# Operand addresses, three more U products ahead, ranks' products on VectorE and another pace of gathers in a PEER layer

## The chip, the cores and the metric

One core of a Trainium2 chip runs the program. The metric is the device time of one execution in microseconds (us): 1605.35 us is the median of three runs of the kernel before (1603.85 to 1605.81).

## What is computed

One encoder layer on 512 tokens of width 1024: a mixer (in-projection, an RG-LRU group, a convolution group, out-projection), then PEER, a retrieval over 128 x 128 single-neuron experts, and a final norm. All is fp32. The part that fills most of the time is PEER:

```python
def peer_ffn(n, w_q, sub_keys, expert_u, expert_v):       # per block of 128 tokens
    q = einsum("td,de->te", xt, w_q)                        # 8 heads x 2 halves x 128
    s = einsum("thpc,hpkc->thpk", q, sub_keys)
    s1, i1 = top_k(s[:, :, 0], 16);  s2, i2 = top_k(s[:, :, 1], 16)
    cand_s = s1[..., :, None] + s2[..., None, :];  cand_i = i1 * 128 + i2
    top_s, pos = top_k(cand_s, 16);  idx = take_along_axis(cand_i, pos);  gate = softmax(top_s)
    act = gelu(einsum("thkd,td->thk", expert_u[idx], xt))
    return einsum("thk,thkd->td", gate * act, expert_v[idx])
```

## The kernel before

**Two ways for the experts.** The first 384 tokens are done densely: all 16384 experts in 128 groups of 128. For group i a *U product* gives gelu(U_i x) for 128 experts x 384 tokens (`dense_u`, L447: 24 matmuls of 384 columns, L452 to L454), the gates are multiplied in (`weigh`, L704), and a *V product* adds V_i times that into six PSUM banks that stay open to the end (`dense_v`, L725: 18 matmuls of 512 columns, L731). The last 128 tokens are done by gathering: 128 (head, rank) pairs, for each a row of U per token and later a row of V per token, 256 "shares" in all. A share is one indirect DMA on POOL's queue into a `g_t` buffer (L655) and one DVE instruction over 128 x 1024 (dots L667, sums L677).

**Precision by splitting.** Each fp32 matrix is loaded by SP's queue into one of five `raw_t` buffers (L94) and split into two fp32r parts: `w_hi` by ACT (L99), `w_lo` by DVE or POOL (L101, the caller chooses). Each product is then three matmul series. The activations are split once, into `m_hi` and `m_lo`.

**Stages.** 0 to about 322 us: mixer. *Routing* to 502.6 us: for the 16 half-heads a query product (`query`, L551, its `w_lo` on POOL), scores, and `rank` on DVE; after half-heads 3, 7 and 11 `choose` (L491) for two heads, after 13 and 15 for one. `choose` finds ranks' keys by comparing with an iota (`eq`, L526 on DVE, 2048 elements for two heads, 1024 for one), multiplying by the index (L528 on POOL, in place) and summing (L530 on DVE), twice. The 22 U products of this stage have their `w_lo` on POOL. *Scatter* to about 680 us: 24 steps build the dense gates by one-hot products (`hot` L623, `oa` L627 on DVE, L633 on PE), write them to memory `scr_g`, and make one U product each, with `w_lo` on DVE, up to U45. *Transition*: gates come back as `g_s` tiles of eight groups (`load_gates`, L699, two buffers), the U products still missing to 48 are made, `w_lo` on POOL. *Main loop* (L750): V0 to V127; in the turns i = 4 to 83 also U(i + 44). *Tail*: the last three V products bank by bank, the norms, the output.

**Homes and pace.** A U product made ahead lives in a home tile until its V product: eight halves of the `g_t` buffers (U0 to U7), 15 `w_e`, 26 `w_f`; HOMES = AHEAD_U + 1 - 8 = 41 in the ring, LAG = 4. The gathers keep a pace: after turn i, `256 * pace(i + 1) // pace(116)` shares are issued, where a turn with U and V counts 2 and one with V alone 1: 2.61 shares in a turn with both, 1.31 in one with V alone, and the last at i = 115.

**Who sets the order.** Each engine runs its own instructions strictly in order; Tile's scheduler fixes that order when the program is built, from the dependences and its own estimate of times. Multiplications by gates (L705) are so drawn far ahead of the loop's turns.

Of the kernel before, what the change touches and what calls it, by code (L numbers as in the profile page):

```python
# [53 lines left out]
SELN = P + 2 + P  # L54


@with_exitstack
def tile_kernel(ctx, tc, x, par, wi, bd, kd, mg, wo, wq, keys, u_rows, v_rows, u_t, v_t, fg, ffg, sel, out):
    nc = tc.nc
# [371 lines left out]
    wk = ctx.enter_context(tc.tile_pool(name="wk", bufs=1))  # L433
    ps_e = ctx.enter_context(tc.tile_pool(name="ps_e", bufs=2, space=PSUM))

    AHEAD_U = 48
    AHEAD_W = 2
    EARLY = 2
    us = {}
# [2 lines left out]
    HOMES_NOW = 15  # L442

    LAG = AHEAD_U - HOMES - 3
    homes = [(wk, "w_e", HOMES_NOW)]

    def dense_u(i, eng):  # L447
        hi, lo = split(load(u_t[i].rearrange("p c e -> p (c e)")), eng)
        p = ps_e.tile([P, TD], F32, name="p_e")
        for c in range(NC):  # L450
            cs = slice(c * P, (c + 1) * P)
            nc.tensor.matmul(p, hi[:, cs], m_hi[:, c, :TD], start=(c == 0), stop=False)  # L452
            nc.tensor.matmul(p, hi[:, cs], m_lo[:, c, :TD], start=False, stop=False)  # L453
            nc.tensor.matmul(p, lo[:, cs], m_hi[:, c, :TD], start=False, stop=(c == NC - 1))  # L454
        if i < len(spare):
            w = spare[i]
        else:
            pool, name, n = homes[(i - len(spare)) % HOMES >= HOMES_NOW]
            w = pool.tile([P, NT, GT], F32, name=name, bufs=n)
        nc.scalar.activation(flat(w), p, AF.Gelu_apprx_tanh)  # L460
        us[i] = w
# [29 lines left out]
    def choose(rp, v, i, g, keys_, h0, n):  # L491
# [32 lines left out]
        for t in range(2):  # L524
            eq = rp.tile(big, BF16, name="eq")
            nc.vector.tensor_tensor(eq, pb[:, t].unsqueeze(1).to_broadcast(big), ioj[:, :, 0:m, :],  # L526
                                    op=ALU.is_equal)
            nc.gpsimd.tensor_tensor(eq, eq, ii[:, :, t, :].rearrange("p h j -> p j h").unsqueeze(3)  # L528
                                    .to_broadcast(big), op=ALU.mult)
            nc.vector.tensor_reduce(merge(keys_[:, t, hh]), eq.rearrange("p j h k -> p h k j"),  # L530
                                    axis=AX.X, op=ALU.add)
# [51 lines left out]


    wk2 = ctx.enter_context(tc.tile_pool(name="wk2", bufs=1))
    homes.append((wk2, "w_f", HOMES - HOMES_NOW))
    TURN = 4
    GS = 8

# [18 lines left out]
    def scatter(b, trb):  # L608

        ahead = None  # L610
        shp = [P, GS // SB, NK, SB]
        for t0 in range(0, P, GT):
            stg = bp.tile([P, NK, GT], F32, name="stg", bufs=2)
            for t1 in range(0, GT, GS):

                def over(q):
                    return (trb[:, q, t0 + t1:t0 + t1 + GS].rearrange("p (g t) -> p g t", t=SB).unsqueeze(2)
                            .to_broadcast(shp))

                hot = []  # L620
                for q in (0, 1):
                    o = bp.tile(shp, BF16, name=f"hot{q}", bufs=2)
                    nc.vector.tensor_tensor(o, iot.unsqueeze(1).to_broadcast(shp), over(q), op=ALU.is_equal)  # L623
                    hot.append(o)
                oa = bp.tile([P, 3] + shp[1:], BF16, name="oa", bufs=2)
                for q in range(3):
                    nc.vector.tensor_tensor(oa[:, q], hot[1], over(2 + q), op=ALU.mult)  # L627
                for t2 in range(0, GS, 4):
                    p = ps_g.tile([P, 4, NK], F32, name="p_g")
                    for t in range(4):  # L630
                        g, o = divmod(t2 + t, SB)
                        for q in range(3):
                            nc.tensor.matmul(p[:, t, :], hot[0][:, g, :, o], oa[:, q, g, :, o],  # L633
                                             start=(q == 0), stop=(q == 2))
                    o = t1 + t2
                    nc.scalar.activation(stg[:, :, o:o + 4], p.rearrange("p t k -> p k t"), AF.Copy)
            nc.sync.dma_start(scr_g[(b * P + t0) // GT], flat(stg))
            if t0 == TURN * GT and b < DB - 1:
                ahead = turned(b + 1)
            if len(us) < AHEAD_U:  # L640
                dense_u(len(us), nc.vector)
        return ahead

# [106 lines left out]
    for i in range(NK):  # L750
# [96 lines left out]
```

## Time and profile before

| what | us |
|---|---|
| median of three runs | 1605.35 |
| the profiled execution | 1603.43 |
| its span (first to last instruction) | 1601.7 |
| PE busy | 1491.6 |
| DVE / POOL / ACT busy | 1225.9 / 649.4 / 637.3 |
| mean granted TensorE clock | 0.964 of 2.4 GHz |

A busy time is the time in which at least one instruction ran on the engine. A wait names what came last before the waiting instruction could start. A profile row of form "A <- B: total, times, longest" is the idle time of A that ended with B.

### The profile page before, as it was taken

How to read it: one execution, taken by the hardware profiler on the slowest of the kernel's cores; microseconds unless marked ns; L12 is line 12 of the kernel's file. 1: busy time of each engine (PE TensorE's matmuls, PEld its weight loads, DVE VectorE, ACT ScalarE, POOL GpSimd, SP SyncE). 2: the span in 40 equal slices, each digit the busy share in tenths (PEclk: the TensorE clock that was granted, in tenths of full speed). 3: DMA queues.
4: the chain of work that ended last, by engine and by line, in shares of the span. 5: the costliest groups of instructions: out<-in, count | busy, mean ns of one | idle time of the engine just before them, and what ended most of it. 6: DMA issues, size and time to landing. Idle time of an engine off the chain costs nothing.

```text
span 1601.7 us, 21647 instructions
## 1 busy us (share of the span) xinstructions
PE 1491.6 (93%) x7939; PEld 1299.6 (81%) x7939; DVE 1225.9 (77%) x2296; ACT 637.3 (40%) x937; POOL 649.4 (41%) x388
## 2 busy tenths in 40 slices
PE   5987989988987999977999999999999999999997
PEld 4754757878877999967888899889998899888886
DVE  6995645398899999937987777777777877777765
ACT  5367453334334554522333333333333333333333
POOL 3644723465572000224444555454444544444410
PEclk9998979999998999998999999999999999999999
DMA  6210503321322555598998988989989898878762
GB/s 230 91 65 15 196 14 132 105 79 67 106 70 102 213 221 211 190 286 305 365 377 304 328 299 310 328 282 334 324 305 334 287 327 286 293 285 296 284 234 79
DMA packets 137787, 358.69 MB, mean 224 GB/s; under 512 B 10064, under 2 KB 59472, under 8 KB 134352
## 3 DMA queue, kind: packets, MB, share of 16 engines
q1 hardware_dynamic: 100240, 222.03, 40.4%
q0 software_dynamic: 36864, 134.23, 22.8%
q8 instruction: 62, 1.02, 0.3%
q10 hardware_dynamic: 576, 1.05, 0.2%
q14 instruction: 45, 0.37, 0.1%
HBM read 327.91 MB, written 29.36 MB: 223 GB/s over the span
## 4 chain that ended last, share of the span: by engine, by line
PE 59%; DVE 7%; DMA 3%; issue 2%; POOL 1%; ACT 0%; DVEq 0%; ACTq 0%; POOLq 0%
PE po L731 31%; PE p_e L454 8%; PE p_e L452 8%; PE p_e L453 8%; PE p_g L633 3%; DVE oa L627 2%; DMA g_t<-in_u_rows,eidx 2%; DMA g_s<-scr_g 2%; DVE hot L623 1%; DVE w_lo L101 1%; DVE g_t L667 0%; POOL g_t L655 0%; DVE key_d L530 0%; DVE w_f L705 0%; DMA raw_t<-in_u_t 0%
## 5 line engine op out<-in xcount | busy, mean ns | idle before, releaser
L99 ACT CAST w_hi<-raw_t 128x1024 fp32r<-128x1024 f32 x302 | 316.1, 1050 | 426.6 <-PE p_e L453 257.5
L454 PE MATMUL p_e<-m_hi,w_lo 128*128 128x384 f32 x1024 | 349.9, 342 | 10.7 <-DVE w_lo L101 10.7
L452 PE MATMUL p_e<-m_hi,w_hi 128*128 128x384 f32 x1024 | 352.2, 344 | 7.0 <-ACT w_e L460 6.2
L453 PE MATMUL p_e<-m_lo,w_hi 128*128 128x384 f32 x1024 | 348.1, 340 | 0.1
L101 POOL TENSOR_TENSOR w_lo<-raw_t,w_hi 128x1024 fp32r<-128x1024 f32 x70 | 177.2, 2543 | 321.3 <-ACT w_hi L99 303.9
L101 DVE TENSOR_TENSOR w_lo<-raw_t,w_hi 128x1024 fp32r<-128x1024 f32 x232 | 280.4, 1219 | 25.1 <-ACT w_hi L99 25.0
L655 POOL DMA_INDIRECT g_t<-in_u_rows,eidx x128 | 197.9, 1546 | 240.8 <-DVE g_t L667 195.5
L655 POOL DMA_INDIRECT g_t<-in_v_rows,eidx x128 | 187.8, 1467 | 222.7 <-DVE acc L677 211.8
L731 PE MATMUL po<-w_hi,wt_hi 128*128 128x512 f32 x768 | 242.8, 395 | 8.9 <-ACT wt_hi L707 8.9
L731 PE MATMUL po<-w_lo,wt_hi 128*128 128x512 f32 x768 | 243.0, 395 | 0.8 <-DVE w_lo L101 0.8
L731 PE MATMUL po<-w_hi,wt_lo 128*128 128x512 f32 x768 | 243.1, 395 | 0.0
L454 PEld LDWEIGHTS p_e<-m_hi,w_lo 128*128 128x128 f32 x1024 | 196.3, 192 | 12.7 <-DVE w_lo L101 12.7
L452 PEld LDWEIGHTS p_e<-m_hi,w_hi 128*128 128x128 f32 x1024 | 196.4, 192 | 11.6 <-ACT w_e L460 6.9
L453 PEld LDWEIGHTS p_e<-m_lo,w_hi 128*128 128x128 f32 x1024 | 196.4, 192 | 4.2 <-DVE m_lo L133 0.4
L667 DVE SCALAR_TENSOR_TENSOR g_t<-g_t,Xg 128x1024 f32<-128x1024 f32 x128 | 152.3, 1221 | 32.4 <-DMA g_t<-in_u_rows,eidx 32.4
L731 PEld LDWEIGHTS po<-w_lo,wt_hi 128*128 128x128 f32 x768 | 143.9, 187 | 36.9 <-DVE w_lo L101 1.5
L731 PEld LDWEIGHTS po<-w_hi,wt_hi 128*128 128x128 f32 x768 | 143.1, 188 | 37.3 <-ACT wt_hi L707 9.2
L731 PEld LDWEIGHTS po<-w_hi,wt_lo 128*128 128x128 f32 x768 | 143.8, 187 | 35.8 <-DVE wt_lo L709 0.4
L677 DVE SCALAR_TENSOR_TENSOR acc<-g_t,dots,acc 128x1024 f32<-128x1024 f32 x127 | 162.3, 1278 | 0.0
L709 DVE TENSOR_TENSOR wt_lo<-w_f,wt_hi 128x384 fp32r<-128x384 f32 x75 | 42.0, 560 | 112.5 <-ACT wt_hi L707 110.2
L707 ACT CAST wt_hi<-w_f 128x384 fp32r<-128x384 f32 x75 | 38.6, 515 | 205.3 <-PE po L731 202.9
L627 DVE TENSOR_TENSOR oa<-hot,trb 128x1024 bf16<-128x1024 bf16 x144 | 90.6, 681 | 0.0
(214 smaller groups left out, 1937.9 us busy)
## 6 DMA issues: line engine op xcount, KB each, us to landing
raw_t<-in_u_t SPq DMA_DIRECT2D x128, 512.0 KB, 5.9
raw_t<-in_v_t SPq DMA_DIRECT2D x128, 512.0 KB, 5.9
scr_g<-stg SPq DMA_DIRECT2D x24, 1024.0 KB, 4.3
g_s<-scr_g SPq DMA_DIRECT2D x16, 1536.0 KB, 16.0
raw_t<-in_wi SPq DMA_DIRECT2D x16, 512.0 KB, 3.9
raw_t<-in_wq SPq DMA_DIRECT2D x16, 512.0 KB, 3.7
raw_t<-in_wo SPq DMA_DIRECT2D x8, 512.0 KB, 5.5
raw_t<-in_kd SPq DMA_DIRECT2D x6, 512.0 KB, 3.7
```

Source lines behind the costliest of these rows:

```text
L99: nc.scalar.copy(hi, t)
L101: eng.tensor_sub(lo, t, f(hi))
L452: nc.tensor.matmul(p, hi[:, cs], m_hi[:, c, :TD], start=(c == 0), stop=False)
L453: nc.tensor.matmul(p, hi[:, cs], m_lo[:, c, :TD], start=False, stop=False)
L454: nc.tensor.matmul(p, lo[:, cs], m_hi[:, c, :TD], start=False, stop=(c == NC - 1))
L627: nc.vector.tensor_tensor(oa[:, q], hot[1], over(2 + q), op=ALU.mult)
L633: nc.tensor.matmul(p[:, t, :], hot[0][:, g, :, o], oa[:, q, g, :, o], start=(q == 0), stop=(q == 2))
L655: nc.gpsimd.indirect_dma_start(out=t, out_offset=None, in_=rows, in_offset=bass.IndirectOffsetOnAxis(ap=eidx[:, k // K, k % K:k % K + 1], ...
L667: nc.vector.scalar_tensor_tensor(t, t, 1.0, Xg, op0=ALU.mult, op1=ALU.mult, accum_out=dots[:, k:k + 1])
L677: nc.vector.scalar_tensor_tensor(acc, t, dots[:, k:k + 1], acc, op0=ALU.mult, op1=ALU.add)
L709: return whi, wlo, nc.vector.tensor_sub(wlo, flat(w), f(whi))
L731: nc.tensor.matmul(po[b][hf], lhs[:, bs], rhs[:, hf * 512:(hf + 1) * 512], start=(i == 0 and n == 0), stop=(i == NK - 1 and n == 2))
```

## The change

Four edits.

1. **Addresses.** `ones` grows from 1 to 32 floats a partition, and a tile `eps_` of 8 floats that nothing reads is put at the other end of SBUF. The tiles behind them (`m_hi`, `m_lo`, `raw_t`, `w_hi`, `w_lo`, `w_e`, `w_f` on one side; `g_t`, `wt_hi`, `wt_lo`, `stg`, `oa`, `eq` on the other) then begin at 0 instead of 32 modulo 64 bytes. Some tiles of the mixer (`recur`'s, the out-projection's `w_hi` and `w_lo`, `h_t`) go from 0 to 32. Two memsets are added.
2. **51 U products ahead** instead of 48: the ring has 44 homes, three of them (`w_g`) in memory that the scatter frees. The scatter still makes U up to U45; the transition makes five (U46 to U50) instead of two; the loop makes 77 instead of 80, in turns 4 to 80.
3. **The ranks' products** (L528, ten instructions: six of 2048 elements, four of 1024) go from POOL to DVE.
4. **Pace.** No share in the first four turns, 7 parts in a turn with U and V, 3 in one with V alone, over `pace(123)` = 7 x 77 + 3 x 42 = 665 parts: 2.69 shares, then 1.155, and the last at i = 122.

```diff
-    ones = keep.tile([P, 1], F32, name="ones")
-    nc.vector.memset(ones, 1.0)
+    ones_ = keep.tile([P, ONEW], F32, name="ones")
+    nc.vector.memset(ones_, 1.0)
+    ones = ones_[:, 0:1]
...
+    edge = ctx.enter_context(tc.tile_pool(name="edge", bufs=1, side="right"))
+    eps_ = edge.tile([P, 8], F32, name="eps_")
+    nc.vector.memset(eps_, EPS)
...
-    AHEAD_U = 48
+    AHEAD_U = 51
...
-            pool, name, n = homes[(i - len(spare)) % HOMES >= HOMES_NOW]
+            k = (i - len(spare)) % HOMES
+            pool, name, n = homes[(k >= HOMES_NOW) + (k >= HOMES - HOMES_END)]
...
-            nc.gpsimd.tensor_tensor(eq, eq, ii[:, :, t, :].rearrange("p h j -> p j h").unsqueeze(3)
+            nc.vector.tensor_tensor(eq, eq, ii[:, :, t, :].rearrange("p h j -> p j h").unsqueeze(3)
...
-            if len(us) < AHEAD_U:
+            if len(us) < AHEAD_U - HOMES_END - 2:
...
-        return i + min(max(i - LAG, 0), NK - AHEAD_U)
+        n = min(max(i - LAG, 0), NK - AHEAD_U)
+        return 7 * n + 3 * max(i - LAG - n, 0)
...
+    wk3 = ctx.enter_context(tc.tile_pool(name="wk3", bufs=1))
+    homes.append((wk3, "w_g", HOMES_END))
...
-            done = 2 * H * K * pace(i + 1) // pace(NK - 12)
+            done = 2 * H * K * pace(i + 1) // pace(NK - 5)
```

**What moves in the queues.** Line numbers of the changed kernel are 9 to 14 higher (L101 is L110, L526 is L537, L528 is L539, L530 is L541, L705 is L717, L709 is L721, L667 is L678). POOL's queue at the first `choose`, before:

```order
L101 TENSOR_TENSOR w_lo<-raw_t,w_hi 128x1024 x2
L533 TENSOR_TENSOR gate_d<-ts 128x128
L538 TENSOR_TENSOR gate_d<-gate_d,den 128x128
L528 TENSOR_TENSOR eq<-eq,ii 128x2048 x2
L101 TENSOR_TENSOR w_lo<-raw_t,w_hi 128x1024 x6
```

After:

```order
L110 TENSOR_TENSOR w_lo<-raw_t,w_hi 128x1024 x2
L544 TENSOR_TENSOR gate_d<-ts 128x128
L549 TENSOR_TENSOR gate_d<-gate_d,den 128x128
L110 TENSOR_TENSOR w_lo<-raw_t,w_hi 128x1024 x6
```

The two products have left the place between the gates and the six `w_lo`. DVE's queue at the same `choose`, before:

```order
L522 TENSOR_TENSOR pf<-pf 128x128
L526 TENSOR_TENSOR eq<-pb,ioj 128x2048
L523 TENSOR_TENSOR pb<-pf 128x128
L482 MAX_INDEX i_1898<-v_1897,s_2475 128x8
L526 TENSOR_TENSOR eq<-pb,ioj 128x2048
```

After:

```order
L533 TENSOR_TENSOR pf<-pf 128x128
L537 TENSOR_TENSOR eq<-pb,ioj 128x2048
L534 TENSOR_TENSOR pb<-pf 128x128
L539 TENSOR_TENSOR eq<-eq,ii 128x2048
L537 TENSOR_TENSOR eq<-pb,ioj 128x2048
L541 TENSOR_REDUCE key_d<-eq 128x128
L539 TENSOR_TENSOR eq<-eq,ii 128x2048
```

The products now stand on DVE between the comparisons and the sums. DVE's queue from the scatter's last step into the loop, before (`g_t` and `w_e` are homes of U products at L705; at L667 `g_t` is a gathered row):

```order
L101 TENSOR_TENSOR w_lo<-raw_t,w_hi 128x1024 x2
L705 TENSOR_TENSOR g_t<-g_t,g_s 128x384 x5
L709 TENSOR_TENSOR wt_lo<-g_t,wt_hi 128x384 x3
L101 TENSOR_TENSOR w_lo<-raw_t,w_hi 128x1024
L705 TENSOR_TENSOR g_t<-g_t,g_s 128x384 x3
L705 TENSOR_TENSOR w_e<-w_e,g_s 128x384
L709 TENSOR_TENSOR wt_lo<-g_t,wt_hi 128x384
L667 SCALAR_TENSOR_TENSOR g_t,dots<-g_t,Xg 128x1024
L101 TENSOR_TENSOR w_lo<-raw_t,w_hi 128x1024
L705 TENSOR_TENSOR w_e<-w_e,g_s 128x384 x3
L667 SCALAR_TENSOR_TENSOR g_t,dots<-g_t,Xg 128x1024
```

After:

```order
L717 TENSOR_TENSOR g_t<-g_t,g_s 128x384 x5
L721 TENSOR_TENSOR wt_lo<-g_t,wt_hi 128x384 x3
L717 TENSOR_TENSOR g_t<-g_t,g_s 128x384 x3
L717 TENSOR_TENSOR w_e<-w_e,g_s 128x384
L110 TENSOR_TENSOR w_lo<-raw_t,w_hi 128x1024
L717 TENSOR_TENSOR w_e<-w_e,g_s 128x384 x7
L110 TENSOR_TENSOR w_lo<-raw_t,w_hi 128x1024 x2
L717 TENSOR_TENSOR w_e<-w_e,g_s 128x384 x3
L721 TENSOR_TENSOR wt_lo<-g_t,wt_hi 128x384
L717 TENSOR_TENSOR w_e<-w_e,g_s 128x384
L110 TENSOR_TENSOR w_lo<-raw_t,w_hi 128x1024
```

The rows' instructions are gone from this stretch (the first two stand behind the seventh `w_lo`), and more multiplications by gates stand ahead of each `w_lo`. On ACT the gelu of U48 stands behind the first three casts `wt_hi` of the loop:

```order
L471 ACTIVATE w_f<-p_e 128x384
L719 CAST wt_hi<-g_t 128x384 x3
L108 CAST w_hi<-raw_t 128x1024
L471 ACTIVATE w_f<-p_e 128x384
L108 CAST w_hi<-raw_t 128x1024
L471 ACTIVATE w_g<-p_e 128x384
```

Before, the last gelu of the transition (U47) stood ahead of those casts. PE has six U products (U45 to U50) between the scatter's last matmul and V0, where it had three.

## Rows read from the trace of the kernel before

**Rows 1.** Windows by stage: length; busy PE, PEld, DVE, ACT, POOL; clock; DMA share; GB/s
```profile
340.00:502.60 162.60, 137.89 (x690) 125.19 (x688) 145.24 (x630) 57.71 (x84) 96.05 (x47) 0.91 0.24 81
502.60:692.00 189.40, 183.83 (x1785) 175.42 (x1785) 174.69 (x271) 93.41 (x175) 12.32 (x3) 0.98 0.56 204
692.00:701.00 9.00, 0.13 (x2) 0.07 (x1) 1.27 (x3) 2.04 (x4) 0.00 (x0) 0.78 1.00 258
701.00:809.00 108.00, 96.44 (x436) 83.58 (x437) 87.04 (x143) 31.68 (x43) 45.14 (x31) 0.94 0.99 331
809.00:1400.00 591.00, 591.00 (x2962) 531.98 (x2961) 451.99 (x572) 209.38 (x285) 277.34 (x185) 1.00 0.89 314
```

**Rows 2.** Waits in routing, 340 to 505 us: total, times, longest
```profile
PE pq L558 <- POOL w_lo L101: 17.8, 3, 6.0
DVE v L478 <- ACT s L573: 13.2, 4, 5.5
```

**Rows 3.** Timeline of PE in routing: start, us, engine, line, operation, [idle before]
```profile
351.75 0.79 PE L558 MATMUL pq<-m_hi,w_lo 128*128 128x512 f32 x1 [5.95 <-POOL w_lo L101]
...
355.72 0.39 PE L558 MATMUL pq<-m_hi,w_lo 128*128 128x512 f32 x1
...
401.96 0.79 PE L558 MATMUL pq<-m_hi,w_lo 128*128 128x512 f32 x1 [5.94 <-POOL w_lo L101]
```

**Rows 4.** Timeline of POOL at the first choose
```profile
345.55 3.84 POOL L528 TENSOR_TENSOR eq<-eq,ii 128x2048 bf16<-128x2048 bf16 x1 [1.16 <-DVE eq L526]
349.34 7.03 POOL L101 TENSOR_TENSOR w_lo<-raw_t,w_hi 128x1024 fp32r<-128x1024 f32 x3
```

**Rows 5.** DVE by form, 340 to 505 us: busy, mean ns
```profile
L530 DVE TENSOR_REDUCE key_d<-eq 128x128 f32<-128x2048 bf16 x6 | 21.6, 3634 | 0.0
L526 DVE TENSOR_TENSOR eq<-pb,ioj 128x2048 bf16<-128x2048 bf16 x6 | 18.1, 3022 | 0.0
...
L530 DVE TENSOR_REDUCE key_d<-eq 128x64 f32<-128x1024 bf16 x4 | 8.1, 2035 | 1.6 <-POOL eq L528 1.6
...
L526 DVE TENSOR_TENSOR eq<-pb,ioj 128x1024 bf16<-128x1024 bf16 x4 | 6.1, 1523 | 0.0
...
L101 DVE TENSOR_TENSOR w_lo<-raw_t,w_hi 128x1024 fp32r<-128x1024 f32 x3 | 3.6, 1215 | 0.0
```

**Rows 6.** Timeline of DVE: comparisons beside an idle and a busy POOL
```profile
339.02 1.43 DVE L526 TENSOR_TENSOR eq<-pb,ioj 128x2048 bf16<-128x2048 bf16 x1
...
340.85 4.62 DVE L526 TENSOR_TENSOR eq<-pb,ioj 128x2048 bf16<-128x2048 bf16 x1
...
493.81 0.68 DVE L526 TENSOR_TENSOR eq<-pb,ioj 128x1024 bf16<-128x1024 bf16 x1
```

**Rows 7.** Timelines at the transition: PE, DVE, ACT, POOL
```profile
700.93 1.22 PE L731 MATMUL po<-w_hi,wt_hi 128*128 128x512 f32 x2 [8.87 <-ACT wt_hi L707]
...
699.73 2.43 DVE L705 TENSOR_TENSOR g_t<-g_t,g_s 128x384 f32<-128x384 f32 x5 [9.61 <-DMA g_s<-scr_g]
...
691.97 1.04 ACT L99 CAST w_hi<-raw_t 128x1024 fp32r<-128x1024 f32 x1 [2.72 <-issue]
692.92 0.48 ACT L460 ACTIVATE w_f<-p_e 128x384 f32<-128x384 f32 x1
700.37 1.41 ACT L707 CAST wt_hi<-g_t 128x384 fp32r<-128x384 f32 x3 [6.96 <-issue]
...
670.61 11.07 POOL L101 TENSOR_TENSOR w_lo<-raw_t,w_hi 128x1024 fp32r<-128x1024 f32 x2 [166.77 <-ACT w_hi L99]
```

**Rows 8.** DVE's waits, 705 to 815 us
```profile
DVE g_t L667 <- DMA g_t<-in_u_rows,eidx: 19.1, 10, 6.6
```

**Rows 9.** Timeline of PE: V12, U57 and V13 begin
```profile
808.25 0.63 PE L731 MATMUL po<-w_hi,wt_hi 128*128 128x512 f32 x2
...
812.45 0.34 PE L452 MATMUL p_e<-m_hi,w_hi 128*128 128x384 f32 x1
...
816.63 0.63 PE L731 MATMUL po<-w_hi,wt_hi 128*128 128x512 f32 x2
```

More of the change, by code (lines that the diff above doesn't have):

```diff
@@ L54 @@
 SELN = P + 2 + P
+ONEW = 32
 @with_exitstack
@@ L444, in tile_kernel @@
     LAG = AHEAD_U - HOMES - 3
+    HOMES_END = 3
     homes = [(wk, "w_e", HOMES_NOW)]
@@ L585, in tile_kernel @@
     wk2 = ctx.enter_context(tc.tile_pool(name="wk2", bufs=1))
-    homes.append((wk2, "w_f", HOMES - HOMES_NOW))
+    homes.append((wk2, "w_f", HOMES - HOMES_NOW - HOMES_END))
     TURN = 4
```

## Prediction

> **What bounds the kernel now.** The windows by stage come first [rows 1]: the reader sees there which engine is full in each. From 809 to 1400 us PE is busy 591.00 of 591.00 us, and a turn with U and V takes 4.20 + 4.18 = 8.38 us [rows 9]. In the scatter (502.6 to 692) PE has 183.8 and DVE 174.7 of 189.4. Neither place has idle PE time to win, so a gain must come from three others: routing (PE 137.9 of 162.6), the transition (0.13 of 9.0), and the loop's first turns, 701 to 809 (96.4 of 108, clock 0.94). The remaining time before is PE work of fixed size: the change neither adds nor drops a matmul.
>
> The waits of routing come next [rows 2]. PE waits 17.8 us, three times, for a `w_lo` from POOL. The timeline shows one of these stalls, 5.95 us, and nine matmuls behind it that take 3.97 us, from 351.75 to 355.72 [rows 3]; at the loop's 4.20/18 = 0.233 us each [rows 9] they would take 2.1. A stall with the slow stretch behind it is thus about 7.8 us, three 23.5. The cause stands on POOL: L528 runs to 349.39, and only then come three `w_lo` [rows 4]. But the stage ends when DVE has made the last keys, since the scatter needs them. DVE is busy 145.2 of 162.6 us there, and its idle time is 13.2 us in the waits [rows 2], 1.6 ahead of a last sum [rows 5] and some 2.6 us of small change. PE's stall is paid by the end only as far as it makes DVE idle.
>
> **Routing, worked out on DVE.** Taken away: (a) idle time, 13.2 us for scores that PE makes late and 1.6 us for a product on POOL, 14.8 in all. It should vanish: from one stall's end to the next (351.75 to 401.96, 50.2 us [rows 3]) PE has 50.2 - 7.8 = 42.4 us of work, and DVE, after the change, 50.2 less 6.6 idle (half of the 13.2, two such periods) and 3.2 contention (below) plus 4.6 of products, 45.0. DVE is then always behind PE. (b) The slow second comparisons: L526 takes 1.43 and 0.68 us beside an idle POOL, 4.62 beside L528 [rows 6]; the ten take 18.1 + 6.1 = 24.2 us [rows 5] where 6 x 1.43 + 4 x 0.68 = 11.3 would do: 12.9. Added: (c) ten products. The trace has none on DVE. The low end is L526's own free price, 11.3 us; the high end L530's, 21.6 + 8.1 = 29.7 [rows 5]. I take twice L101's 1.215 us for 1024 elements less its fixed part, 2.3 us for 2048 and 1.2 for 1024, because that row too has two inputs and no reuse of a pair of 16-bit elements, as the product, whose index stands still along the last axis, has none: 6 x 2.3 + 4 x 1.2 = 18.6. The Trainium skill, "VectorE: DVE Perf Modes" (What auto-detection actually checks; The TRN2 errata) has the double rate of two-input operations only where every tensor is 16-bit with step 1, and (N + 151)/0.96 ns at the single rate, an estimate of 2.29 us for 2048; the sum would be the same, and no row here shows it. Net: -14.8 - 12.9 + 18.6 = **-9.1**, ends -16.4 and +2.0. POOL keeps making 24 `w_lo` in this stage and may now meet the products; I give back 1 and take **-8**. What is late next is DVE itself: PE stands at the end of routing and waits for the first gates, so the 23.5 us are not had whole.
>
> **Transition and first turns, worked out on PE and checked on DMA.** PE ends U47 at 692.1 and starts V0 at 700.93; DVE gets the gates at 699.73, ACT casts them at 700.37 [rows 7]. The change puts U48 to U50 into this hole. Their `w_lo` come from POOL in time: the first two of the transition end at 681.7 [rows 7], three more at 7.03/3 = 2.34 us each [rows 4] make it 689. U48 and U49 fill 692.1 to 700.4. U50 needs a PSUM bank (there are two) that the gelu of U48 frees, and this gelu stands on ACT behind three `wt_hi` (700.37 + 1.41), a `w_hi` (1.04) and itself (0.48): about 703.3 [rows 7]. So a wait of 2.9 us stays, U50 ends near 707.5, and V0 starts at about 708 with three U products more behind it (3 x 4.18 = 12.5 us).
>
> From there the count goes to the 14th turn, i = 13, because PE never idles after it. Before, its U57 starts at 812.45 [rows 9]. After, turn 13 has U60; without any stall it would start at 708 + 4 x 4.20 + 9 x 8.38 = 800.2. Since U57 to U59 are done then as well, "no gain" would be 812.45 + 12.5 = 825.0, and the upper end of the gain is 24.8 us. What stood in the way before: in 701 to 809 DVE waits 19.1 us, ten times, for gathered rows [rows 8], and the `w_lo` that PE needs stand behind; the 11.6 us of idle PE and the slower clock follow [rows 1]. After, no row is consumed until turn 4. But DMA is full all through, 1.00 and 0.99 of its time at 258 and 331 GB/s [rows 1]. So the bytes are counted in the order of the queue. Up to the `w_lo` of turn 13's U, DVE needs before: 23 `w_lo` (0.52 MB of matrix each), 7 tiles `g_s` (1.57 MB), 28 rows (0.52 MB): 37.7 MB. After: 23, 8 and 24: 37.2 MB. On a full DMA turn 13 comes no earlier than before, by bytes: gain 12.5, because three U products less remain. That is the lower end. The last 2 to 3 MB of the stretch are loaded ahead of need (five `raw_t`, four `g_t` buffers), worth up to 2.5/0.331 = 7.6 us. Between 12.5 and 24.8 I take **-15**, near the end that the full DMA sets.
>
> **The rest.** Steady loop: 2.69 instead of 2.61 shares are 0.04 MB a turn; a turn moves 2 x 0.524 + 2.69 x 0.524 + 1.57/8 = 2.65 MB, 317 GB/s, where DMA was busy 0.89 at 314 [rows 1], so PE covers it: 0. DVE gets a twelfth of a share more a turn with 452 of 591 us busy [rows 1]: 0. Turns with V alone have 1.155 instead of 1.31 shares, but seven turns longer; PE is bound there, and the last share is consumed five V products (21 us) before the end: 0. Two memsets at the start: 0. Scatter: untouched, 0. Alignment: nearest rows are the U and V matmuls, 4.18/24 = 0.174 us for 384 columns and 0.233 for 512 [rows 9], where the columns alone at 2.4 GHz are 0.160 and 0.213. Nothing in the trace ties the 13 and 20 ns to an address, so I take 0; the bounds are 0 and all of it, 3072 x 0.0135 + 2304 x 0.020 = 87 us. A loss is less likely, since the tiles that leave a multiple of 64 bytes are in the mixer's small operations.
>
> Sum: -8 - 15 = -23 against the profiled execution, 1603.43 to 1580.4. The median of the runs lies 1.9 above that execution, so I forecast **1582**. Its own range is 1605.35 less 41 (16.4 + 24.8) to less 8 (no routing gain beyond 2 lost, 12.5, and some 2 us of disturbance): 1564 to 1597.
>
> **The rivals.**
> 1. *Alignment makes matmuls shorter.* For it: the 13 and 20 ns are there in every matmul, and every fixed operand stood at 32 modulo 64. Against: the two sizes of overhead differ though the addresses do not. Half of it would be another 43 us: 1539. The Trainium skill, "TensorE: Matmul & The Clock Gate" (Wait — 56ns, not 53.3ns?) has N/2.4 GHz plus 2.5 ns as the spacing of matmuls; rows 9 disagree with 0.174 and 0.233 us. If an address were the reason and the page's spacing came back, 3072 x 0.011 + 2304 x 0.0175 = 74 us would go: 1508.
> 2. *The products on DVE are dear.* If each costs what a comparison beside a reading POOL costs, 4.62 us, 2.3 for the small ones [rows 6, 5], the ten are 37 us, the chain gets 9 longer instead of 8 shorter, and the time is 1599. It decides from 27.7 us for the ten. For it: POOL's `w_lo` has two inputs, and beside the scatter's products two of them took 11.07 us [rows 7] instead of 4.7 [rows 4]. Against: of ten comparisons those without L528 beside them were free. By the Trainium skill, "SBUF — State Buffer" (Who interferes with whom), an instruction of VectorE with two SBUF inputs contends with a GpSimd instruction that reads SBUF, which speaks for this rival; the 4.62 beside 1.43 us agree with it.
> 3. *The gates come too late in the first turns.* More L705 stand ahead of each `w_lo`: by turn 8 DVE has to have 13 matrices, 7 `g_s` and 10 rows (23 MB) instead of 13, 4 and 15 (21 MB). If `w_lo` queue behind `g_s`, turn 13 comes at some 820 and the two terms give 5 instead of 15: 1592.
> 4. *DMA becomes the bound of the loop, and the kernel is slower.* At less than 317 GB/s the 77 turns grow; at 300 they take 2.65/0.300 = 8.84 us, 36 us in all: 1618. It beats the gains from 305 GB/s down (8.69 us, 24 us). Against: the first turns moved 331.
> 5. *U48 to U50 do not fill the hole* (their operands late, or PE's order held by a bank): V0 at 713, no term but routing and what DMA leaves: 1591.
>
> **How the numbers follow.** Forecast 0.55, alignment 0.12, dear products 0.12, late gates 0.12, DMA 0.07, hole 0.02. The range leaves out the half-price alignment and the DMA case, 0.19: from 1556 (the forecast's low end and a small part of rival 1) to 1600. A measurement of this kernel tells 0.2%, 3 us, from no change, so faster is below 1602.1: all of the forecast and of rivals 1, 3, 5 (0.81) and 0.07 of rival 2: 0.88. The rest of rival 2 is the same, 0.05; rival 4 is slower, 0.07.
>
> **What would show it.** Routing: PE no longer waits for a POOL `w_lo` at L558's place, DVE has no idle over 1 us between 340 and its last key, the product's mean is near 2.3 us, and the last key comes near 494 instead of 502. Transition: PE's wait ahead of U50 or V0 is about 3 us instead of 8.87. First turns: DVE's wait for rows is nearly gone, one for `g_s` may be new, and PE is unbroken from turn 13, U60 near 802 on the old clock of the trace less 8. Loop: 8.38 us a turn; 8.3 or less means that alignment counts, more than 8.4 that DMA does. Wrong would be a routing stage of old length, or a turn 13 as late as before with 12.5 us not won.

## The result, and the profile after

The changed kernel takes 1582.37 us in the median of four runs (1580.88 to 1583.92), the kernel before 1605.58 on the same chip: a ratio of 0.9863, 95% interval 0.9851 to 0.9874. The forecast was 1582, in a range of 1556 to 1600. The total is right, but it is not made of the parts that the prediction added up: one part came about as forecast, one hardly at all, and one that was put at nothing took its place.

The profiled execution of the changed kernel has a span of 1579.1 us against 1601.7. The windows by stage, with the columns of [rows 1]:

```profile
340.00:502.60 162.60, 136.16 (x693) 123.71 (x691) 160.15 (x641) 59.16 (x86) 74.94 (x37) 0.93 0.25 85
502.60:692.00 189.40, 183.66 (x1782) 175.38 (x1782) 170.37 (x267) 91.71 (x172) 16.84 (x5) 0.97 0.57 201
692.00:701.00 9.00, 9.00 (x53) 8.82 (x51) 1.87 (x4) 2.71 (x5) 2.46 (x2) 1.00 1.06 274
701.00:809.00 108.00, 99.27 (x466) 88.11 (x466) 85.46 (x139) 35.08 (x48) 40.50 (x27) 0.95 1.06 354
809.00:1400.00 591.00, 591.00 (x2971) 535.87 (x2971) 463.24 (x586) 210.47 (x287) 288.50 (x191) 1.00 0.90 316
```

The hole of the transition (third row) is full. Routing (first row) still ends where it did, with DVE now busy for 160 of 162.6 us instead of 145 and PE as idle as before. From 809 us on PE was full before and is full now, and yet that part has become shorter. The timeline of PE of the changed kernel has the points that tell the stages apart: the first transposition of gates (routing is over), U50, U60 of turn 13, and the begins of two V products in the turns with V alone.

```profile
502.42 0.47 PE L611 MATMUL p_e<-ident,src 128*128 128x128 f32 x1 [8.44 <-ACT src L610]
...
702.57 0.44 PE L462 MATMUL p_e<-m_hi,w_hi 128*128 128x384 f32 x1 [1.43 <-ACT w_f L471]
...
811.12 0.33 PE L462 MATMUL p_e<-m_hi,w_hi 128*128 128x384 f32 x1
...
1413.05 0.62 PE L745 MATMUL po<-w_hi,wt_hi 128*128 128x512 f32 x2
...
1417.17 0.62 PE L745 MATMUL po<-w_hi,wt_hi 128*128 128x512 f32 x2
```

The same points from the timelines of both kernels:

| point on PE | before | after |
|---|---|---|
| first query product | 280.64 | 281.08 |
| routing over, first transposition of gates | 502.62 | 502.42 |
| U45, the scatter's last | 679.34 | 680.09 |
| V0 | 700.93, behind U47 | 706.85, behind U50 |
| turn 13 begins | 812.45 (U57) | 811.12 (U60) |
| a turn with U and V; with V alone | 8.380; 4.20 | 8.307; 4.12 |
| span | 1601.7 | 1579.1 |

Up to U45 nothing is won (0.75 us lost, with 0.4 of later start). From U45 to turn 13: 811.12 - 680.09 = 131.0 us against 812.45 - 679.34 + 12.5 = 145.6 (the 12.5 us are the three U products that are done by then now): 14.6 us won. From there to the end, 768.0 us against 776.8: 8.8 won. -14.6 - 8.8 + 0.75 = -22.6, the difference of the spans.

### The profile page after: what moved, and what is told of

It is laid out like the page before. It is cut to its first block, busy times and chain, and to the rows that moved or that the text cites. A ratio compares the mean times of both kernels' runs of the same rounds, so it can differ in the third digit from the quotient of the medians.

```text
span 1579.1 us, 21654 instructions
## 1 busy us (share of the span) xinstructions
PE 1479.1 (94%) x7939; PEld 1299.8 (82%) x7939; DVE 1234.1 (78%) x2304; ACT 634.8 (40%) x937; POOL 639.4 (40%) x381
## 4 chain that ended last, share of the span: by engine, by line
PE 68%; DVE 23%; issue 3%; DMA 3%; ACT 2%; POOL 1%; SPq 0%; DVEq 0%; ACTq 0%; POOLq 0%
PE po L745 31%; PE p_e L462 9%; PE p_e L464 9%; PE p_e L463 9%; DVE oa L638 2%; PE p_g L644 2%; DVE key_d L541 2%; DMA g_s<-scr_g 2%; DVE hot L634 2%; DVE w_lo L110 1%; DVE eq L539 1%; DVE eq L537 1%; DVE pc L228 1%; PE pz L417 1%; PE pz L418 1%
## 5 line engine op out<-in xcount | busy, mean ns | idle before, releaser
L110 POOL TENSOR_TENSOR w_lo<-raw_t,w_hi 128x1024 fp32r<-128x1024 f32 x73 | 194.4, 2677 | 335.0 <-ACT w_hi L108 335.0
L666 POOL DMA_INDIRECT g_t<-in_u_rows,eidx x128 | 199.9, 1562 | 226.2 <-DVE g_t L678 171.9
L110 DVE TENSOR_TENSOR w_lo<-raw_t,w_hi 128x1024 fp32r<-128x1024 f32 x229 | 276.6, 1220 | 12.4 <-ACT w_hi L108 12.4
L745 PE MATMUL po<-w_lo,wt_hi 128*128 128x512 f32 x768 | 238.9, 390 | 0.9 <-DVE w_lo L110 0.9
L745 PE MATMUL po<-w_hi,wt_lo 128*128 128x512 f32 x768 | 239.4, 391 | 0.0
L678 DVE SCALAR_TENSOR_TENSOR g_t<-g_t,Xg 128x1024 f32<-128x1024 f32 x128 | 151.9, 1222 | 16.7 <-DMA g_t<-in_u_rows,eidx 16.7
L719 ACT CAST wt_hi<-w_f 128x384 fp32r<-128x384 f32 x69 | 35.4, 513 | 183.0 <-PE po L745 183.0
L721 DVE TENSOR_TENSOR wt_lo<-w_f,wt_hi 128x384 fp32r<-128x384 f32 x69 | 38.6, 559 | 88.2 <-ACT wt_hi L719 87.8
```

Of the source, the lines that this page charges most:

```text
L110: eng.tensor_sub(lo, t, f(hi))
L666: nc.gpsimd.indirect_dma_start(out=t, out_offset=None, in_=rows, in_offset=bass.IndirectOffsetOnAxis(ap=eidx[:, k // K, k % K:k % K + 1], ...
L678: nc.vector.scalar_tensor_tensor(t, t, 1.0, Xg, op0=ALU.mult, op1=ALU.mult, accum_out=dots[:, k:k + 1])
L719: nc.scalar.copy(whi, flat(w))
L721: return whi, wlo, nc.vector.tensor_sub(wlo, flat(w), f(whi))
L745: nc.tensor.matmul(po[b][hf], lhs[:, bs], rhs[:, hf * 512:(hf + 1) * 512], start=(i == 0 and n == 0), stop=(i == NK - 1 and n == 2))
```

## The experiments

Ratios are to the kernel before, run beside each on the same chip; the intervals are 95%.

**The addresses alone.** The two edits of part 1 put into the kernel before, together (e1) and one at a time (e2, e3):

```diff
-    ones = keep.tile([P, 1], F32, name="ones")
+    ones_ = keep.tile([P, 32], F32, name="ones")          # e1, e2
...
+    edge = ctx.enter_context(tc.tile_pool(name="edge", bufs=1, side="right"))
+    eps_ = edge.tile([P, 8], F32, name="eps_")            # e1, e3
```

Expected of e1:

> The kernel before with edit 1 alone (ones of 32 floats, the unread tile of 8 floats); every engine's queue keeps its order but for the memset. In the trace of the changed kernel the V matmuls start 226 to 227 ns apart where they started 233 before, and a V takes 4.12 us instead of 4.20. Theory: the addresses do that by themselves. Then 128 V at 0.08 us less are 10 us: 1595, a V turn of 4.12 us, U matmuls still 173 ns apart. Rival: the shorter V comes with another edit (fewer rows beside V, another place of the homes). Then no change, 1605, and 4.20 us.

Measured: 1594.64 us, ratio 0.9944 (0.9927 to 0.9960); a V alone 4.12 us, which is 229 ns a matmul and not the 226 to 227 expected, a turn with U and V 8.307, U matmuls 173 ns apart as before. The rival falls: every engine's queue in this trace is that of the kernel before but for the memsets, so the shorter V is the addresses' doing.

> The kernel before with only ones of 32 floats: the tiles of the left side (the moving w_hi and w_lo of a V product, and both operands of a U product) go from 32 to 0 modulo 64 bytes, the stationary wt_hi and wt_lo of a V product stay at 32. Theory moving operand: all of the gain, 1595, V 4.12 us. Theory stationary operand: none of it, 1605, V 4.20 us. Theory both: a part, or none unless the other side moves too.

Measured: 1604.00, ratio 0.9996 (0.9986 to 1.0005). The begins of V90 and V91 in its timeline are 4.20 us apart:

```profile
1433.17 0.63 PE L732 MATMUL po<-w_hi,wt_hi 128*128 128x512 f32 x2
...
1437.38 0.63 PE L732 MATMUL po<-w_hi,wt_hi 128*128 128x512 f32 x2
```

> The kernel before with only the unread tile of 8 floats: the tiles of the right side (the stationary wt_hi and wt_lo of a V product, the gathered rows, the gates) go from 32 to 0 modulo 64 bytes, the moving w_hi and w_lo stay at 32. Theory stationary operand: all of the gain, 1595, V 4.12 us. Theory moving operand: none, 1605, V 4.20 us.

Measured: 1604.61, ratio 0.9996 (0.9987 to 1.0006), V 4.20 us. Neither side alone gives anything, both together 10 us: it is a matter of the pair. Two readings were left, and e8 tells them apart: both operands have to begin at a multiple of 64 bytes, or they have to stand right to each other. It leaves the left side where it was and moves the right side by 64 bytes, so that both stand at 160 modulo 256, not at a multiple of 64:

```diff
+    eps_ = edge.tile([P, 16], F32, name="eps_")
```

> The kernel before with an unread tile of 16 floats on the right side: the stationary wt_hi and wt_lo of V then stand at 160 modulo 256 bytes, as the moving w_hi and w_lo do, both at 32 modulo 64. Moving either side alone to a multiple of 64 bytes gave nothing, both together 0.08 us a V. Theory multiples of 64: both have to be at one, so nothing: V 4.20 us, 1604. Rival, the distance: what counts is how the two operands stand to each other modulo 256 (64 apart before and after, so this alone can't be it) or that they are equal, as in the in-projection whose matmuls start 227 ns apart with both at 160: V 4.1 us, 1592 to 1595.

Measured: 1594.71, ratio 0.9928 (0.9911 to 0.9944); V alone 4.08 us. Multiples of 64 are not needed: two operands at an odd place, but the same one, are faster than the changed kernel's. e9 moves the pool of the gates alone:

```diff
     ws = {i: weigh(i, us.pop(i)) for i in range(AHEAD_W)}
+    pad_ = gq.tile([P, 16], F32, name="pad_", bufs=1)
```

> The kernel before with an unread tile of 16 floats in the pool of the gates alone: only wt_hi, wt_lo, acc, dots and g_s move by 64 bytes (wt_hi and wt_lo from 224 to 160 modulo 256); the gathered rows, stg, eq and every tile of the left side keep their place. Theory: the two operands of a V matmul decide; with both at 160 the V is short: 4.08 us in turns with V alone, 1594 to 1596. Rival: another tile that moved along (gathered rows, stg) made the V short: 4.20 us, 1604 to 1606.

Measured: 1595.56, ratio 0.9938 (0.9918 to 0.9959). V90 and V91 begin 4.08 us apart:

```profile
1429.20 0.62 PE L733 MATMUL po<-w_hi,wt_hi 128*128 128x512 f32 x2
...
1433.28 0.62 PE L733 MATMUL po<-w_hi,wt_hi 128*128 128x512 f32 x2
```

So the gathered rows, `stg` and the whole left side have nothing to do with it; of the tiles that did move (`wt_hi`, `wt_lo`, `acc`, `dots`, `g_s`) only the first two are operands of a V matmul. All cases, with the places as the program lays them out:

| kernel | moving w_hi, w_lo, modulo 256 | stationary wt_hi, wt_lo | V alone, us | turn with U and V |
|---|---|---|---|---|
| before | 160 | 224 | 4.20 | 8.380 |
| e2 | 0 | 224 | 4.20 | 8.380 |
| e3 | 160 | 192 | 4.20 | 8.380 |
| after, e1 | 0 | 192 | 4.12 | 8.307 |
| e8, e9 | 160 | 160 | 4.08 | 8.307 |
| e10, e11 | 192 | 192 | 4.08 | 8.310, 8.308 |

In U products both operands stand at one place in all kernels (160 before, 0 after, 192 in e10), and they are 173 ns apart in all. In the slow pair of 160 and 224 the moving operand stands 64 bytes behind the stationary one, in the nearly good pair of 0 and 192 it stands 64 ahead modulo 256; no run tries these two distances with the stationary operand elsewhere.

The trace of the kernel before held an answer that was not read. In the mixer's convolution group the moving operand goes 4 bytes further from tap to tap (46 taps in two series), while the stationary one stays at 160. From the timeline of PE, the first matmul of three taps, with the moving operand at 160, 164 and 168:

```profile
98.55 0.39 PE L233 MATMUL pc<-g_hi,w_hi 128*128 128x512 f32 x1
...
99.22 0.40 PE L233 MATMUL pc<-g_hi,w_hi 128*128 128x512 f32 x1
...
99.93 0.39 PE L233 MATMUL pc<-g_hi,w_hi 128*128 128x512 f32 x1
```

A tap is three matmuls. At 160 and 160 they start 227, 227 and 226 ns apart, at 164 and 160 it is 237, 232 and 238, and the medians of all other taps lie between 229 and 240. The changed kernel, with the stationary operand at 0, and e10, with it at 192, give nearly the same numbers at the same distance: 227, 227 and 226 at distance 0, and 234, 233 and 232 in the changed kernel at 128 and 0, both multiples of 64. So it is the distance modulo 256 bytes that counts there, and only the tap at equal places has the short spacing in all three matmuls.

**The ranks' products alone (e4):** `nc.gpsimd` becomes `nc.vector` at L528, nothing else.

> The kernel before with edit 3 alone (the ranks' products on DVE). Theory from the trace of the changed kernel: DVE loses its idle time in routing but gets as much work back, since its comparisons, products and sums are long beside POOL's w_lo; the last keys come 1 to 2 us earlier and the time is 1603 to 1606. Rival, the step of the prediction: 8 us less, 1597. Second rival: the products alone are worth more than in the changed kernel, because there the other edits disturb routing: under 1597.

Measured: 1605.21, ratio 1.0006 (0.9996 to 1.0015): nothing, in either direction. In its timeline PE waits for the first gates until 502.07, 8.44 us:

```profile
502.07 0.47 PE L600 MATMUL p_e<-ident,src 128*128 128x128 f32 x1 [8.44 <-ACT src L599]
```

**Homes and pace, one at a time.** e5 has 51 U products ahead with the old pace, e6 the new pace with 48.

```diff
-    AHEAD_U = 48
+    AHEAD_U = 51        # e5, with the homes w_g and the scatter's limit
...
-        return i + min(max(i - LAG, 0), NK - AHEAD_U)
+        return 7 * n + 3 * max(i - LAG - n, 0)        # e6, with pace(NK - 5)
```

> The kernel before with edit 2 alone: 51 U products ahead, the old rule of the pace (2.65 shares in a turn with U and V, 1.33 with V alone). Theory: the three U products fill the hole of the transition, but V0 to V3 stand behind gathered rows as before and DMA is as full as before, so turn 13 comes at the old time with three U products less behind it: 12.5 us less, 1593. Rival 1: the pace does the work; with rows in the first turns the gain of the hole is given back there: above 1600. Rival 2: the homes give all of it and the pace nothing: 1591 or less.

Measured: 1602.90, ratio 0.9981 (0.9968 to 0.9994), 3 us and not 12.5. Rival 1 is right. V0 comes at 710.16, 29.0 us after U45 (26.8 in the changed kernel), but then the timelines of POOL, DVE and PE and three windows of the trace (columns of [rows 1]) show this:

```profile
704.54 4.65 POOL L657 DMA_INDIRECT g_t<-in_u_rows,eidx  x1 [7.24 <-DVE wt_lo L711]
...
716.85 1.23 DVE L669 SCALAR_TENSOR_TENSOR g_t<-g_t,Xg 128x1024 f32<-128x1024 f32 x1 [8.67 <-DMA g_t<-in_u_rows,eidx]
...
720.68 1.22 PE L735 MATMUL po<-w_lo,wt_hi 128*128 128x512 f32 x2 [5.70 <-DVE w_lo L101]
...
708.20:716.90 8.70, 6.78 (x30) 5.53 (x28) 0.05 (x1) 2.95 (x4) 0.99 (x1) 0.95 1.07 321
716.90:720.70 3.80, 0.02 (x1) 0.02 (x1) 3.80 (x7) 0.00 (x0) 1.01 (x1) 0.83 0.27 51
720.70:730.00 9.30, 9.30 (x29) 7.43 (x30) 8.50 (x15) 1.51 (x2) 2.99 (x2) 0.70 0.92 275
```

POOL asks for the first gathered row at 704.54, once `wt_lo` has read the row's `g_t` buffer; DVE stands 8.67 us before it, the `w_lo` of the second V product stands behind it in DVE's queue, and PE gives back 5.70 us of the hole. In that wait DMA is full (321 GB/s; the row shares it with a `g_s` tile of 1.5 MB). In the next 3.8 us it is nearly idle (0.27 busy, 51 GB/s): SP loads no matrix until DVE has made that `w_lo` and so freed a `raw_t` buffer. The mean granted clock of the 9.3 us behind it is 0.70, between the two levels of 1.2 and 2.4 GHz. Turn 13 (U60) comes at 822.39, 141.2 us after U45.

> The kernel before with edit 4 alone: 48 U products ahead, no share in the first four turns, then 7 to 3 parts, last at i = 122. The hole of 8.9 us stays. Theory: DMA is full in the first turns and its bytes up to turn 13 stay nearly the same (23 matrices, 28 rows before, 24 after), so at most 4 rows, 2 MB or 6 us, are won: 1599 to 1604. Rival: the rows that DVE waited for were the cause by themselves: 10 us or more, under 1595.

Measured: 1597.60, ratio 0.9945 (0.9928 to 0.9961): 8.6 us, between the theory and its rival and nearer to the rival. The hole stays, and then PE runs through to 758 us:

```profile
701.94 1.22 PE L732 MATMUL po<-w_hi,wt_hi 128*128 128x512 f32 x2 [8.82 <-ACT wt_hi L708]
...
758.38 0.49 PE L452 MATMUL p_e<-m_hi,w_hi 128*128 128x384 f32 x1 [3.35 <-ACT w_e L460]
```

Addresses 10, pace 8.6, homes 3.3, products 0: their sum is 22, and the four together gave 23. Each has an interval of 1.5 to 2.7 us to either side, so no interplay of the four is shown, and a small one is not excluded.

**Is DVE the bound of routing? (e7, on the changed kernel.)** The ten sums become four halvings each:

```diff
-            nc.vector.tensor_reduce(merge(keys_[:, t, hh]), eq.rearrange("p j h k -> p h k j"),
-                                    axis=AX.X, op=ALU.add)
+            for w in (8, 4, 2):
+                nc.vector.tensor_tensor(eq[:, 0:w], eq[:, 0:w], eq[:, w:2 * w], op=ALU.add)
+            nc.vector.tensor_tensor(merge(keys_[:, t, hh]), eq[:, 0], eq[:, 1], op=ALU.add)
```

> The changed kernel with the ten sums over 16 ranks (3.84 and 1.85 us each, 30 us in all) made as four halvings by additions of 16-bit tiles (1024, 512, 256, 128 elements; exact, since each sum has one term that is not zero). Theory: routing is bound by DVE in the changed kernel, 160 of 162.6 us busy, so what DVE saves comes off the end until PE is the bound: a tree takes 0.7 + 0.4 + 0.3 + 0.3 us, 16 us less in all, PE has some 20 us of idle time there: 1568 to 1573. Rival: the additions have two inputs in SBUF and get long beside POOL's w_lo as comparisons and products do, half the gain: 1574 to 1577. Second rival: routing's end is not set by DVE: 1582.

Measured: 1587.45, ratio 0.9885 (0.9868 to 0.9901): 3 to 4 us slower than the changed kernel by the ratios, outside all three expectations. DVE by form, 325 to 510 us, and then, from the timelines of DVE and POOL, single additions and a product of the first `choose`:

```profile
L539 DVE TENSOR_TENSOR eq<-eq,ii 128x2048 bf16<-128x2048 bf16 x6 | 20.3, 3375 | 0.0
...
L542 DVE TENSOR_TENSOR eq<-eq 128x512 bf16<-128x512 bf16 x10 | 10.7, 1073 | 0.0
L542 DVE TENSOR_TENSOR eq<-eq 128x1024 bf16<-128x1024 bf16 x6 | 10.6, 1770 | 0.0
L542 DVE TENSOR_TENSOR eq<-eq 128x256 bf16<-128x256 bf16 x10 | 7.2, 717 | 0.0
...
346.85 2.88 DVE L542 TENSOR_TENSOR eq<-eq 128x1024 bf16<-128x1024 bf16 x1
349.66 4.47 DVE L539 TENSOR_TENSOR eq<-eq,ii 128x2048 bf16<-128x2048 bf16 x1
...
356.59 0.68 DVE L542 TENSOR_TENSOR eq<-eq 128x1024 bf16<-128x1024 bf16 x1
357.94 2.48 DVE L542 TENSOR_TENSOR eq<-eq 128x256 bf16<-128x256 bf16 x1
...
341.44 10.55 POOL L110 TENSOR_TENSOR w_lo<-raw_t,w_hi 128x1024 fp32r<-128x1024 f32 x3 [1.34 <-ACT w_hi L108]
357.70 2.56 POOL L110 TENSOR_TENSOR w_lo<-raw_t,w_hi 128x1024 fp32r<-128x1024 f32 x1 [1.32 <-ACT w_hi L108]
```

An addition of 1024 elements takes 1.77 us in the mean where its free price is 0.68, and the six products next to them went from 2.69 to 3.38 us. Sums that read one tile were replaced by instructions that read two, and these meet POOL's `w_lo`. The single lines show what a meeting costs: 2.88 instead of 0.68 us, 4.47 instead of 2.28, and 2.48 for 256 elements, which take 0.28 alone. That is 2.2 us each time, whatever the size and close to one `w_lo` (7.03/3 = 2.34 us on POOL [rows 4]), so four short additions are four chances to pay it. From the first query product to the transposition of gates routing takes 507.60 - 281.36 = 226.2 us, 4.9 more than in the changed kernel, and the end follows: DVE does set routing's end.

**Two ways to beat both kernels.** e10 is the changed kernel with ONEW = 16, so that both operands of V stand at 192; e11 adds four more turns without rows:

```diff
-ONEW = 32
+ONEW = 16
...
-        n = min(max(i - LAG, 0), NK - AHEAD_U)
+        n = min(max(i - LAG - 4, 0), NK - AHEAD_U - 4)        # e11; the same 4 in the line behind
```

> The changed kernel with ones of 16 floats instead of 32: w_hi, w_lo and wt_hi, wt_lo all at 192 modulo 256 bytes, where the changed kernel has 0 and 192. Theory that equal places modulo 256 are what counts and that 64 apart on a multiple of 64 is only the second best: V alone 4.08 us instead of 4.12, 51 V at 0.04 us are 2 us less than the changed kernel: ratio to before 0.985. Theory multiples of 64 bytes: the same as the changed kernel, 4.12 us, ratio 0.9863. Rival: turns with U and V get longer, since U's operands move too: over 0.9863.

Measured: 1582.32, ratio 0.9856 (0.9837 to 0.9874). V alone takes 4.08 us as expected, but the 2 us are within the interval: unclear in the time, clear in the trace. From turn 13 to the end this trace needs 766.4 us, 1.6 less than that of the changed kernel; from U45 to turn 13 it needs 134.1, 3.1 more, with the same order of work.

> The kernel of the run before, and the rows of the gathers kept back for four turns more: none in the first eight turns, then 7 to 3 parts (2.81 shares in a turn with U and V), last at i = 122. Theory: in the first turns of the changed kernel the rows, the gates and the matrices share a full DMA, so keeping 11 rows back lets the gates come earlier: of the 9 us of PE's waits there some 3 to 6 go, 1574 to 1578. Rival 1: these waits are for gates whatever the rows do: 1580. Rival 2: 2.81 shares a turn fill DMA in the steady turns: the turn gets longer than 8.31 us and the time is 1584 or more.

Measured: 1573.66, ratio 0.9802 (0.9782 to 0.9821), 8.7 us less than e10 and just below the range of the theory. In 701 to 809 us PE is busy 104.0 us instead of 96.1 in e10 (99.3 in the changed kernel):

```profile
701.00:809.00 108.00, 104.00 (x503) 92.84 (x502) 81.87 (x130) 38.29 (x53) 27.75 (x19) 0.97 1.02 323
```

One wait of PE for a `w_lo`, of 2.0 us, is left in these turns, where e10 has 6.8 us of them. The step of the theory is not what the trace shows: the gates come no earlier, DVE waits 14.3 us for the later ones as in e10 (14.2). What is gone is ten rows, their 5.7 MB and their ten instructions ahead of the `w_lo`. Turn 13 (U60) comes at 805.95, 124.2 us after U45, and the steady turn keeps its 8.308 us with 2.81 shares, so the second rival falls.

e12 tests the reading of e7 the other way round, on top of e11: of each pair of products the first stays on DVE and the second goes back to POOL, beside the sum that reads one tile.

```diff
-            nc.vector.tensor_tensor(eq, eq, ii
+            (nc.vector, nc.gpsimd)[t].tensor_tensor(eq, eq, ii
```

> The kernel of e11 with the second of each pair of ranks' products on POOL again (five of ten: three of 2048 elements, two of 1024) and the first on DVE. On POOL the second product runs while DVE makes the first sum, which reads one tile only. Theory: DVE sets the end of routing and pays for its two-input instructions beside POOL's; five products less are 3 x 2.69 + 2 x 1.2 = 10.5 us of DVE, of which its wait for POOL at the second sum gives some back: the last keys 4 to 8 us earlier than in the changed kernel (502.4 is where the gates' transposition begins), 1566 to 1570. Rival 1: POOL's w_lo come later again and PE stalls, and DVE waits for scores as in the kernel before: 1573, no change. Rival 2: the second sum waits for the whole POOL queue: slower than 1575.

Measured: 1560.51, ratio 0.9727 (0.9711 to 0.9743): 12 us beyond e11, more than expected. Its timeline on DVE and POOL at the first `choose`, and PE at the end of routing:

```profile
350.10 3.86 DVE L541 TENSOR_REDUCE key_d<-eq 128x128 f32<-128x2048 bf16 x1
354.16 3.84 DVE L541 TENSOR_REDUCE key_d<-eq 128x128 f32<-128x2048 bf16 x1 [0.20 <-POOL eq L539]
...
350.26 3.87 POOL L539 TENSOR_TENSOR eq<-eq,ii 128x2048 bf16<-128x2048 bf16 x1 [1.16 <-DVE eq L537]
...
494.95 0.48 PE L611 MATMUL p_e<-ident,src 128*128 128x128 f32 x1 [7.45 <-ACT src L610]
```

The product on POOL and the first sum on DVE run side by side at their free prices, 3.87 and 3.86 us. From the first query to the transposition of gates routing takes 494.95 - 284.65 = 210.3 us; in the changed kernel 502.42 - 281.08 = 221.3, before 222.0. The 11 us are found on DVE: its products fell from 21.0 to 9.3 us (five left, and the three of 2048 that stayed take 2.28 us now), the short comparisons from 4.9 to 2.7, against 1.2 us of new waits for POOL's products and 1.5 for a `w_hi`.

## Why the prediction was right, and where not

**Routing: forecast -8, measured -0.6** (222.0 to 221.3 us from the first query to the gates). The mechanism was named: DVE's chain ends the stage, PE's 23.5 us of stalls are not had whole, and PE would wait for the first gates at the end. It does, 8.44 us. DVE's idle time went as forecast: no wait for scores is left among its waits from 340 to 505 us, of which this is the largest:

```profile
DVE ts L489 <- POOL cs L514: 1.5, 2, 0.8
```

PE did not stop waiting for POOL's `w_lo`, as the prediction's sign had it: 7.3 us in two waits are left of 17.8. By the prediction's own words, "wrong would be a routing stage of old length", this part was wrong. The step that failed is the contention: 12.9 us from freed comparisons, and "I give back 1" for the products. DVE by form, 340 to 505 us:

```profile
L541 DVE TENSOR_REDUCE key_d<-eq 128x128 f32<-128x2048 bf16 x6 | 23.0, 3835 | 0.0
L539 DVE TENSOR_TENSOR eq<-eq,ii 128x2048 bf16<-128x2048 bf16 x6 | 16.1, 2688 | 0.0
L537 DVE TENSOR_TENSOR eq<-pb,ioj 128x2048 bf16<-128x2048 bf16 x6 | 14.4, 2404 | 0.0
...
L541 DVE TENSOR_REDUCE key_d<-eq 128x64 f32<-128x1024 bf16 x4 | 7.8, 1950 | 0.0
L537 DVE TENSOR_TENSOR eq<-pb,ioj 128x1024 bf16<-128x1024 bf16 x4 | 4.9, 1225 | 0.0
```

The comparisons lost 24.2 - 19.3 = 4.9 us, not 12.9, and the products cost 21.0, not 18.6: 10.4 us given back where 1 was put. Sums that take 1 us more and small items that take less make up the rest. The reason is seen at the first `choose`, DVE and POOL:

```profile
341.03 2.28 DVE L539 TENSOR_TENSOR eq<-eq,ii 128x2048 bf16<-128x2048 bf16 x1
343.23 3.42 DVE L537 TENSOR_TENSOR eq<-pb,ioj 128x2048 bf16<-128x2048 bf16 x1
...
350.37 3.07 DVE L539 TENSOR_TENSOR eq<-eq,ii 128x2048 bf16<-128x2048 bf16 x1
...
341.17 10.12 POOL L110 TENSOR_TENSOR w_lo<-raw_t,w_hi 128x1024 fp32r<-128x1024 f32 x3 [1.35 <-ACT w_hi L108]
```

With L528 gone from POOL, the `w_lo` behind it move forward into exactly the place where DVE compares and multiplies, and they contend as L528 did: three take 10.12 us instead of 7.03 [rows 4], the second comparison 3.42 instead of 1.43, the second product 3.07 instead of 2.28. The first product, which began 0.14 us ahead of the `w_lo`, kept its 2.28; in these rows it is the later one that gets longer. I had freed the comparisons of L528 and not asked what POOL does instead. The product's free price was right (2.28 and 1.22 us for 2.3 and 1.2); its mean, 2.69, is between the forecast and rival 2, which had the mechanism and a price that was too high. The Trainium skill, "SBUF — State Buffer" (Who interferes with whom), says that a two-input instruction of VectorE contends with a GpSimd instruction that reads SBUF and that a reduction does not; e7 and e12 agree with both halves, 1.77 us for 0.68 in the one, 3.86 beside 3.87 us in the other.

**Transition and first turns: forecast -15, measured -14.6** from U45 to turn 13, of which some 1 us belongs to the addresses (13 V at 0.08). That is one execution: the same stretch of e7 and e10, with the same homes and pace, gives 12.5 and 11.5 (133.1 and 134.1 us), so the term is right to some 3 us. The chain at U50 was right: it waits for the gelu of U48, 1.43 us instead of 2.9, and V0 comes at 706.85 instead of 708. The floor under this term, "on a full DMA turn 13 comes no earlier than before, gain 12.5", was no floor: it took 331 GB/s for what a full DMA moves, and the same window moved 354 after the change. The bytes that DMA moved from U45 to turn 13 and the times are:

| kernel | MB | us | GB/s |
|---|---|---|---|
| e11 | 38.9 | 124.2 | 313 |
| e6 | 41.0 | 125.6 | 327 |
| before | 42.5 | 133.1 | 319 |
| after | 44.6 | 131.0 | 340 |
| e5 | 45.5 | 141.2 | 322 |

With the homes alone (e5) the gain is 145.6 - 141.2 = 4.4 us; with the rows held back (e11) it is 145.6 - 124.2 = 21.4, near the 24.8 that was the ceiling. The changed kernel, e5 and e11 make three U products more in this stretch than the other two. Two readings are left. One is the prediction's: the fewer bytes, the earlier turn 13, and the table keeps that order except for the changed kernel. The other is the order in DVE's queue: what stands ahead of a `w_lo` delays it, as at the stall of e5, where DMA, too, came to stand nearly idle behind it. Every run that took rows out of the first turns took both, their bytes and their place in the queue, so how much belongs to each is not shown. Rival 3, the late gates, is in the trace of the changed kernel and costs some of it: among the waits from 660 to 830 us, and in one that PE pays for, since the `w_lo` stands behind the gates in DVE's queue:

```profile
DVE w_f L717 <- DMA g_s<-scr_g: 8.4, 3, 6.4
...
PE p_e L464 <- DVE w_lo L110: 6.3, 3, 3.0
DVE g_t L678 <- DMA g_t<-in_u_rows,eidx: 5.6, 6, 2.1
...
DVE w_e L717 <- DMA g_s<-scr_g: 5.5, 1, 5.5
...
763.76 0.56 DVE L717 TENSOR_TENSOR w_f<-w_f,g_s 128x384 f32<-128x384 f32 x1 [6.40 <-DMA g_s<-scr_g]
...
768.27 0.45 PE L464 MATMUL p_e<-m_hi,w_lo 128*128 128x384 f32 x1 [2.29 <-DVE w_lo L110]
```

The 19.1 us of waits for rows [rows 8] are 5.6 now, and 13.9 us of waits for the later gates stand in their place; PE waits 6.3 us instead of 10.7 for a `w_lo` of a U product.

**Addresses: forecast 0, measured -10** (0.9944 alone). "Nothing in the trace ties the 13 and 20 ns to an address" looks true for each operand by itself, and I had looked at them one by one. The pair was not looked at: in the kernel before, the in-projection and the U and query products had both operands at one place and 13 ns of overhead, the V products and nearly all of the mixer's convolution products had two places and some 20. That trace did tie the spacing to an address, in the taps shown above. 4.20 to 4.12 us is 4.4 ns a matmul, a fifth of that overhead. The argument against rival 1, that the overheads differ though the addresses do not, was wrong in its second half: modulo 64 the places were equal, modulo 256 they were not.

**The rest.** Steady turns stayed PE-bound at 2.69 shares and at 316 GB/s; rival 4 did not come. Rival 5 did not either. The total was right because -8 that did not come and -10 that was not forecast nearly cancel: without the addresses the measured parts come to some 1590, still inside the range. The middle was hit by luck.

## What to carry to other kernels

When an instruction is taken off one engine, look at what moves into its place in that engine's queue before counting its neighbours as free: here the same contention came back from the next instruction. Pair a two-input instruction on one of VectorE and GpSimd with a one-input reduction on the other (e12), and keep optional loads out of the turns right after a hole, since both their bytes and their place ahead of a needed operand in an in-order queue can cost there (e5, e6, e11; not told apart). Compare matmul spacings between products of one shape in the same trace: a difference between 227 and 233 ns, and a product whose operand moves by 4 bytes a step, were there to be read.

## What was not expected of the hardware

The spacing of 512-column fp32r matmuls depends on the places of the moving and the stationary operand together: 4.08 us for 18 with both at 160 or both at 192 modulo 256 bytes, 4.12 at 0 and 192, 4.20 at 160 and 224, 0 and 224, 160 and 192. The convolution taps agree: 227 ns at equal places, 229 to 240 at 45 other distances. Moving the stationary operand's pool alone by 64 bytes (e9) is worth 10 us of this kernel. And replacing a reduction of 3.84 us by four smaller additions, 1.7 us at free prices, made it slower beside a busy GpSimd (e7), since a VectorE instruction with two inputs that met a `w_lo` on GpSimd got up to 2.2 us longer, the short ones as much as the long.
